# Filler gate weights of a hybrid encoder block: high and low parts made by GpSimd's converting and accumulating DMAs and a negated copy, instead of a load, a ScalarE copy and a VectorE subtraction

## The chip, the cores and the metric

The kernel runs on one core of a Trainium2 chip. A core has a matrix engine (TensorE, PE in the profile, with its weight loads as PEld), VectorE (DVE), ScalarE (ACT), GpSimd (POOL) and SyncE (SP), which here only issues DMAs. The engines work in parallel, each through its own instruction queue in order, and wait for one another by semaphores. The metric is the device time of one execution in microseconds (us).

## What is computed

One layer of an encoder with 1024 tokens and model width 1024, in float32. The reference, cut to what matters here:

```python
hn = rms_norm(x, norm_mix_g)
u = hn @ w_in                               # w_in: 1024 x 7864
u_mla, u_fox, u_ssm, u_gate = jnp.split(u, split_at, axis=-1)
y_a = mla_branch(u_mla, ...) @ w_br_mla     # attention, 8 heads
y_b = fox_branch(u_fox, ...) @ w_br_fox     # attention with decay, 8 heads
y_c = ssm_branch(u_ssm, ...) @ w_br_ssm     # Mamba-2 scan in chunks
g = sigmoid(u_gate + b_gate).reshape(B, S, 3, D)
x = x + (g[:, :, 0] * y_a + g[:, :, 1] * y_b + g[:, :, 2] * y_c) @ w_out
x = x + conv_ffn(rms_norm(x, norm_ffn_g), ...)
```

The part at issue is `u_gate`: 1024 tokens by 3 x 1024 gate columns, of which the last 3072 columns of `w_in` are the weights.

## The kernel before

**Arithmetic in two parts.** TensorE works on a rounded float32 type, `fp32r`. To keep float32 accuracy every operand `a` is split into a high part `h`, which is `a` rounded to `fp32r`, and a low part `l = a - h`. A product takes three matmuls, high by high, high by low, low by high. `hnh` and `hnl` are the two parts of the normalised input, transposed, in halves of 512 tokens; `wh` and `wl` are those of the weights.

**The stages, in order.** Projections (0 to some 380 us of the profile), the convolution's products with two pairs of gate blocks and a last single block, the bridge (L1481, to 531.8 us), attention of the 16 heads (to some 872), the chunk-wise SSD scan (to some 1066), the three branches' output products (L2328), the output product, and the gated MLP.

**The filler.** The gate columns come in 24 blocks of 128. Four are done earlier; the other 20 are the filler: a generator, `all_fill`, hands out their matmuls (L1588) in small groups that are placed between the matmuls of attention and of the scan, so that TensorE has work while the other engines do softmax and scan steps. A block is 48 matmuls of 128 x 512, in two halves of 512 tokens, each ended by a tanh on ScalarE (L1566) and, after the second, a store by SP (L1598). Per block of the rows `k = 0 .. 7`, the order is `wh·hnh`, `wh·hnl`, `wl·hnh`: the third matmul of a block is the first that reads `wl`.

**Loading a block.** `fill_load` is called for block n+1 when block n begins. It takes a raw buffer (`wr`), starts one 512 KB load on SP (L1552), and plans a ScalarE copy that rounds into `wh` (L1559) and a VectorE subtraction into `wl` (L1560). `wh` and `wl` have two buffers each, so the buffer of block n+1 is the one that block n-1 has used. The raw buffers, two as well, come free earlier: their load can run while TensorE still reads the `wh` of the same turn. The first two blocks are loaded with `now=True`, before the first attention matmul, with the helper `split` (L134, L135).

**What sets the order.** In attention the order on PE, ACT, DVE and POOL is worked out at build time by a planner (`Sim`): a list of tasks, each with an engine, the time for which it occupies it, the time until its result is there, and the tasks it follows. In this mode `later(us, fn, eng, cost, after)` adds such a task. In the scan only PE's order is written by hand; `later` then puts its work at so many microseconds of the builder's own clock behind the call, and the framework's scheduler orders ACT, DVE and POOL, with `pin` keeping those filler instructions in program order. GpSimd's own work in attention is the normalisation of the softmax rows (`pm`, L1926), between the exponential on ScalarE (L1918, with its row maximum `nmx` and reciprocal `rs` on DVE) and the transposes on PE (`tp`, L1966). In the scan it is, for each chunk, two products (`xdd` L2127, `y` L2129) and a chain of eight small operations for a reciprocal root (`yv` L2196 to `yr` L180). `xdd` is split by ScalarE (`xddh`) and VectorE (`xddl`) for the next chunk's state product (`pst`).

## Time and profile before

| | us |
|---|---|
| median of 3 runs | 1977.04 (1975.92 to 1977.86) |
| the profiled execution | 1973.83 |
| its span | 1972.1 |
| PE busy | 1949.2 (99%) |
| DVE, ACT, POOL busy | 1401.0, 976.9, 699.9 |
| TensorE clock granted | 0.999 |

The span is the time from the first to the last instruction of the profiled execution. Busy times are sums over instructions; matmuls are pipelined and their ends modelled, so that neighbouring ones overlap (one of 128 x 512 is listed at 390 ns, and the next starts 227 ns later). Instructions that issue a DMA aren't counted as busy. A wait is put down to the releaser that came last. In timelines the columns are the start, the duration, the engine, the line and what it writes and reads, and in brackets the idle time ahead of it with its releaser.

### The profile page before, as it was taken

The numbers are of one execution on the slowest core, as the hardware profiler recorded it, in microseconds if no ns is written. First come the engines' busy times: TensorE is split into PE (matmuls) and PEld (weight loads), VectorE is DVE, ScalarE is ACT, GpSimd is POOL, SyncE is SP. The second block draws the span as 40 slices with busy tenths as digits, with TensorE's granted clock in tenths as the row PEclk, the third lists the DMA queues.
The fourth block names the chain that finished last, engine by engine and source line by source line (L and its number), as shares of the span: only waits on it lengthen the run. The fifth ranks groups of instructions, "written<-read, shape, count | busy, mean of one in ns | idle before, by whom it ended". The sixth has DMA issues, their size and how long they took to land.

```text
span 1972.1 us, 28446 instructions
## 1 busy us (share of the span) xinstructions
PE 1949.2 (99%) x10053; PEld 1658.6 (84%) x10053; DVE 1401.0 (71%) x2178; ACT 976.9 (50%) x1690; POOL 699.9 (35%) x666
## 2 busy tenths in 40 slices
PE   9999999999999999999999999999999999999999
PEld 8989878888899988887888888888878888888887
DVE  7777769579566676758884575568997877765555
ACT  5555324454566666657783222225544444444432
POOL 5133100166133333213331451102664454423665
PEclk9999999999999999999999999999999999999999
DMA  6166755532757666635646875434222211259575
GB/s 181 53 198 212 202 132 155 187 102 91 227 167 195 177 179 169 170 95 194 214 152 228 291 252 184 139 107 127 94 90 86 76 53 54 86 166 337 185 262 191
DMA packets 281673, 318.46 MB, mean 161 GB/s; under 512 B 19405, under 2 KB 209497, under 8 KB 281530
## 3 DMA queue, kind: packets, MB, share of 16 engines
q1 hardware_dynamic: 281528, 316.64, 51.6%
q8 instruction: 79, 1.29, 0.3%
q14 instruction: 64, 0.52, 0.1%
q10 hardware_dynamic: 2, 0.00, 0.0%
HBM read 223.46 MB, written 93.13 MB: 161 GB/s over the span
## 4 chain that ended last, share of the span: by engine, by line
PE 86%; DVE 5%; issue 3%; ACT 2%; DMA 2%; POOL 1%; SPq 1%; ACTq 0%; DVEq 0%; POOLq 0%
PE dn L2760 10%; PE mm L1588 10%; PE ybr L2328 7%; PE cb L1384 7%; PE ua L2419 6%; PE uc L2419 5%; PE ud L2419 5%; PE wo L2464 4%; PE s L1899 4%; PE fx L798 3%; PE fx L1134 3%; PE tp L1966 3%; PE ub L2419 2%; PE fxv L188 2%; PE py L2172 1%
## 5 line engine op out<-in xcount | busy, mean ns | idle before, releaser
L2760 PE MATMUL dn<-dr,dr 128*128 128x512 f32 x592 | 182.3, 389 | 0.0
L1926 POOL TENSOR_SCALAR pm<-pm,rs 128x128 f32<-128x128 f32 (+7 forms) x128 | 95.3, 747 | 227.1 <-DVE rs L1924 203.6
L1588 PE MATMUL mm<-hnh,wh 128*128 128x512 f32 x320 | 132.6, 414 | 0.3 <-ACT t L1566 0.3
L2760 PEld LDWEIGHTS dn<-dr,dr 128*128 128x128 f32 x592 | 111.2, 188 | 22.9
L1588 PE MATMUL mm<-hnh,wl 128*128 128x512 f32 x320 | 125.7, 393 | 0.0
L1918 ACT ACTIVATE pm<-s,nmx 128x128 f32<-128x128 f32 (+7 forms) x128 | 94.8, 741 | 61.6 <-DVE nmx L1913 52.3
L1588 PE MATMUL mm<-hnl,wh 128*128 128x512 f32 x320 | 125.2, 391 | 0.0
L2760 PE MATMUL dn<-dr 128*128 128x512 f32 x296 | 115.3, 390 | 0.0
L1974 DVE TENSOR_TENSOR ptl<-tp,pth 128x512 fp32r<-128x512 f32 (+1 forms) x160 | 96.8, 632 | 23.7 <-ACT pth L1970 22.4
L135 DVE TENSOR_TENSOR dr<-dr,dr 128x1024 fp32r<-128x1024 f32 x52 | 71.4, 1380 | 51.7 <-ACT dr L134 44.4
L135 DVE TENSOR_TENSOR wl<-S,wh 128x1024 fp32r<-128x1024 f32 x55 | 81.4, 1480 | 35.6 <-ACT wh L134 35.5
L1913 DVE TENSOR_REDUCE nmx<-s 128x1 f32<-128x128 f32 (+7 forms) x128 | 93.4, 748 | 16.0 <-PE s L1899 9.3
L2328 PE MATMUL ybr<-ah,wl 128*128 128x512 f32 x256 | 99.8, 390 | 0.7 <-DVE wl L135 0.7
L2328 PE MATMUL ybr<-al,wh 128*128 128x512 f32 x256 | 99.9, 390 | 0.0
L2328 PE MATMUL ybr<-ah,wh 128*128 128x512 f32 x256 | 99.7, 390 | 0.0
L134 ACT ACTIVATE wh<-wr 128x1024 fp32r<-128x1024 f32 (+1 forms) x47 | 42.4, 902 | 104.6 <-PE ybr L2328 41.2
L1970 ACT ACTIVATE pth<-tp 128x512 fp32r<-128x512 f32 (+1 forms) x160 | 82.7, 553 | 23.1 <-PE tp L1966 21.2
L134 ACT ACTIVATE wh<-S 128x1024 fp32r<-128x1024 f32 x55 | 58.3, 1059 | 67.4 <-PE uc L2419 45.9
L134 ACT ACTIVATE dr<-dr 128x1024 fp32r<-128x1024 f32 x52 | 54.9, 1060 | 71.8 <-PE dn L2760 52.9
L1966 PE MATMUL tp<-ident,pm 128*128 128x128 f32 x576 | 80.9, 273 | 0.2 <-POOL pm L1926 0.2
L135 DVE TENSOR_TENSOR wl<-wr,wh 128x1024 fp32r<-128x1024 f32 (+1 forms) x47 | 54.5, 1159 | 32.9 <-ACT wh L134 32.8
L2637 DVE SCALAR_TENSOR_TENSOR fa<-cg,pc_f,fa 128x1023 f32<-128x1023 f32 (+1 forms) x44 | 74.2, 1688 | 1.4 <-ACT fa L2632 1.4
(665 smaller groups left out, 6219.4 us busy)
## 6 DMA issues: line engine op xcount, KB each, us to landing
dr<-act_d SPq DMA_DIRECT2D x99, 256.0 KB
wr<-in_w_in_dram SPq DMA_DIRECT2D x35, 512.0 KB
raw<-in_w_in_dram SPq DMA_DIRECT2D x27, 512.0 KB
gl<-g_d SPq DMA_DIRECT2D x24, 512.0 KB
wr<-in_ffn_w_up_dram SPq DMA_DIRECT2D x23, 512.0 KB
ws<-in_ffn_w_down_dram SPq DMA_DIRECT2D x22, 512.0 KB
wsum_d<-ws SPq DMA_DIRECT2D x22, 512.0 KB
act_d<-fa SPq DMA_DIRECT2D x22, 512.0 KB
```

Of the source, the lines that this page charges most:

```text
L134: i = A.activation(h, src, AF.Copy) if he is A else he.tensor_copy(h, src)
L135: return i, le.tensor_sub(l, src, f32(h))
L1384: T.matmul(ps, a, b, start=first and i == 0, stop=i == 11, skip_group_check=not first)
L1588: T.matmul(ps, a[:, k, :], b[half][:, k, :], start=(k == 0 and i == 0), stop=(k == NK - 1 and i == 2))
L1913: V.reduce_max(r.nmx[:, 0:1], r.row, axis=AX, negate=True)
L1918: A.activation(r.p[:, 0:cols], r.row, AF.Exp, bias=r.nmx[:, 0:1], accum_out=r.rs[:, 0:1])
L1926: r.norm = Task("G", (d - 0.025, d), lambda: G.tensor_scalar(r.p[:, 0:cols], r.p[:, 0:cols], r.rs[:, 1:2], 0.0, op0=ALU.mult, op1=ALU.add) ...
L1966: T.transpose(x.pt[:, c * P:c * P + P], rows_[qi].p[:, k * P:k * P + P], ident)
L1974: V.tensor_sub(x.tl[:, :off], x.pt[:, :off], f32(x.th[:, :off]))
L2328: T.matmul(pss[half], w_[:, k, :], a_[k][:, hs], start=k == 0 and i == 0, stop=k == nk - 1 and i == 2)
L2419: T.matmul(ps, a, b, start=first and n == 0, stop=n == 11, skip_group_check=not first)
L2760: T.matmul(ps[m], a[:, ts_], b[:, 512:], start=first_ and j == 0 and q == 0, stop=j == NFH - 1 and q == 2, skip_group_check=not first_)
```

## The change

For each filler block the raw buffer, SP's load, and VectorE's subtraction go. GpSimd instead starts two DMAs that read the weights' DRAM columns and write `wh`, rounding to `fp32r` on the way, four rows `k` each (256 KB). ScalarE writes `-h` into `wl`. GpSimd then starts four DMAs, of two rows `k` each (128 KB), that read the same DRAM columns again and add them to `wl`, so that it holds `w - h`. In the first two blocks this is issued at once; in the others the two, the one and the four are tasks, each after the one before.

```diff
     def fill_load(c0, now=False):
-        raw, rl = f_wr.get()
-        SY.dma_start(raw, w_inv[:, :, c0:c0 + P])
+        src = w_inv[:, :, c0:c0 + P]
         h, _ = f_wh.get()
-        l, _ = f_wl.get()
+        l, rl = f_wl.get()
         if now:
-            split(h, l, raw)
+            for k in (0, 4):
+                G.dma_start(h[:, k:k + 4, :], src[:, k:k + 4, :])
+            A.activation(l, f32(h), AF.Copy, scale=-1.0)
+            for k in (0, 2, 4, 6):
+                G.dma_start(l[:, k:k + 2, :], src[:, k:k + 2, :], accum_op=ALU.add)
             rl[0] = None
             return h, l, rl
-        i = later(4.0, lambda: pin(A.activation(h, raw, AF.Copy)), "A", (0.95, 1.06))
-        rl[0] = later(5.3, lambda: pin(V.tensor_sub(l, raw, f32(h))), "V", (1.13, 1.22), [i])
+        hd = None
+        for k in (0, 4):
+            hd = later(0.5, lambda k=k: pin(G.dma_start(h[:, k:k + 4, :], src[:, k:k + 4, :])), "G", (1.3, 5.0), hd and [hd])
+        rl[0] = later(7.0, lambda: pin(A.activation(l, f32(h), AF.Copy, scale=-1.0)), "A", (0.95, 1.06), [hd])
+        for k in (0, 2, 4, 6):
+            rl[0] = later(9.0, lambda k=k: pin(G.dma_start(l[:, k:k + 2, :], src[:, k:k + 2, :], accum_op=ALU.add)), "G", (1.0, 5.0), [rl[0]])
         return h, l, rl
```

Behind the change lines are seven higher: L1588 is L1595 there, L1926 is L1933, L2127 is L2134.

GpSimd's queue at the start of attention. Before, the last sum of the convolution (`cv`) is followed by the normalisations:

```order
L1459 TENSOR_TENSOR cv_5760<-X_5746,e_1084_5692 128x512
L1926 TENSOR_SCALAR pm_5909<-pm_5909,rs_5910 128x128
L1926 TENSOR_SCALAR pm_5912<-pm_5912,rs_5913 128x256
L1926 TENSOR_SCALAR pm_5933<-pm_5933,rs_5934 128x384
L1926 TENSOR_SCALAR pm_5947<-pm_5947,rs_5948 128x512
```

Now the DMAs of the first two blocks stand between:

```order
L1459 TENSOR_TENSOR cv_5760<-X_5746,e_1084_5692 128x512
L1556 DMA wh_5865<-in_w_in_dram 128x4x128 x2
L1559 DMA wl_5866<-in_w_in_dram 128x2x128 x4
L1556 DMA wh_5874<-in_w_in_dram 128x4x128 x2
L1559 DMA wl_5875<-in_w_in_dram 128x2x128 x4
L1933 TENSOR_SCALAR pm_5915<-pm_5915,rs_5916 128x128
L1933 TENSOR_SCALAR pm_5918<-pm_5918,rs_5919 128x256
```

Twelve DMAs have moved ahead of the first `pm`; the third pair, `wh_5874`, is written to the buffer that the bridge's matmuls read last.

ScalarE's queue at the same place, before, from the last tanh of the convolution's gates (`cv`) to the first exponential (`pm`):

```order
L1467 ACTIVATE cv_5760<-cv_5760,pc_g 128x1024
L1484 ACTIVATE gb_5774<-cb_5775,pc_g 128x512
L134 ACTIVATE wh_5873<-wr_5871 128x1024
L1484 ACTIVATE gb_5774<-cb_5801,pc_g 128x512
L1918 ACT_TABLE_LOAD
L1918 ACTIVATE pm_5909,rs_5910<-s_5891,nmx_5899 128x128
```

and now:

```order
L1467 ACTIVATE cv_5760<-cv_5760,pc_g 128x1024
L1557 ACTIVATE wl_5866<-wh_5865 128x1024
L1484 ACTIVATE gb_5774<-cb_5775,pc_g 128x512
L1484 ACTIVATE gb_5774<-cb_5801,pc_g 128x512
L1557 ACTIVATE wl_5875<-wh_5874 128x1024
L1925 ACT_TABLE_LOAD
L1925 ACTIVATE pm_5915,rs_5916<-s_5897,nmx_5905 128x128
```

Both blocks' copies have moved back: the first behind the tanh of `cv`, the second to the place right ahead of the first exponential.

GpSimd's queue in the scan. Before, the end of one chunk's chain (`yr`), the next chunk's products, and the next chain's first operation:

```order
L180 TENSOR_SCALAR yr_2552_11387<-rg_t_11396,yr_2552_11387 128x1
L179 TENSOR_SCALAR rg_t_11399<-yr_2552_11387,rg_v_11391 128x1
L180 TENSOR_SCALAR yr_2552_11387<-rg_t_11399,yr_2552_11387 128x1
L2127 TENSOR_TENSOR xdd_11558<-xT_11432,dend 128x1024
L2129 TENSOR_TENSOR y_11560<-xT_11432,Db 128x1024
L2196 TENSOR_SCALAR yv_2607_11607<-yss_11604 128x1
```

Now, at a chunk of the scan's first half:

```order
L180 TENSOR_SCALAR yr_2505_11190<-rg_t_11202,yr_2505_11190 128x1
L1567 DMA wl_11094<-in_w_in_dram 128x2x128 x4
L1564 DMA wh_11318<-in_w_in_dram 128x4x128 x2
L2134 TENSOR_TENSOR xdd_11363<-xT_11235,dend 128x1024
L2136 TENSOR_TENSOR y_11365<-xT_11235,Db 128x1024
L2203 TENSOR_SCALAR yv_2564_11413<-yss_11410 128x1
```

Six DMAs stand between the chain and `xdd`; from the fourth block of the scan on it is the two of `wh` that stand there, and the four of `wl` stand behind `y`.

## The prediction

> **What bounds the kernel now.** First the page: the busy line and the chain of waits.

> ```profile
> span 1972.1 us, 28446 instructions
> PE 1949.2 (99%) x10053; PEld 1658.6 (84%) x10053; DVE 1401.0 (71%) x2178; ACT 976.9 (50%) x1690; POOL 699.9 (35%) x666
> PE 86%; DVE 5%; issue 3%; ACT 2%; DMA 2%; POOL 1%; SPq 1%; ACTq 0%; DVEq 0%; POOLq 0%
> ```

> TensorE is without work for 1972.1 - 1949.2 = 22.9 us in all, so no relief of another engine can win more than that. The change touches the stretch in which the filler runs, attention (about 530 to 870 us) and the SSD scan (870 to 1070). Next, therefore, the waits of PE in those two windows:

> ```profile
> PE o L1978 <- DVE o L1950: 1.0, 4, 0.3
> PE s L1899 <- ACT pm L1918: 0.4, 2, 0.2
> PE tp L1966 <- POOL pm L1926: 0.2, 1, 0.2
> ...
> PE pst L2146 <- DVE xddl L135: 2.0, 1, 2.0
> PE stp L2104 <- issue: 1.3, 1, 1.3
> PE mm L1588 <- ACT t L1566: 0.3, 1, 0.3
> ```

> The columns are total us, times, longest. They add up to 5.2 us in 540 us: here TensorE alone sets the pace, and only 1.0 + 2.0 = 3.0 us hang on DVE, the engine that the change relieves. The other engines by window (us of PE, PEld, DVE, ACT, POOL, then clock, DMA share, GB/s):

> ```profile
> 650.00:700.00 50.00, 49.25 (x328) 44.41 (x326) 35.79 (x73) 33.90 (x75) 20.86 (x23) 1.00 0.67 187
> 950.00:970.00 20.00, 20.00 (x118) 17.30 (x117) 17.29 (x25) 16.26 (x36) 7.48 (x11) 1.00 0.65 198
> ```

> In attention GpSimd is free for 29.1 of 50 us; in one scan chunk of 20 us DVE is free for 2.7, ScalarE for 3.7 and GpSimd for 12.5.

> **What is removed.** For each of 20 blocks:

> ```profile
> L1552 SPq DMA_DIRECT2D wr<-in_w_in_dram x20: 373/384/592, 496.3 to 1011.9; - x20
> L1559 ACT ACTIVATE wh<-wr x18: 1042/1052/1069, 571.1 to 1038.4; 128x1024 fp32r<-128x1024 f32 x18
> L1560 DVE TENSOR_TENSOR wl<-wr,wh x18: 1205/1216/2928, 572.2 to 1045.7; 128x1024 fp32r<-128x1024 f32 x18
> ```

> DVE loses 20 x 1.216 = 24 us and SP 20 x 0.38 = 8 us, both beside TensorE's work. ScalarE keeps one pass of about 1.05 us per block, the negated copy, of the same size. What of it is on the path shows at the first scan chunk, where `pst` waited 2.0 us for `xddl`:

> ```profile
> 892.01 2.93 DVE L1560 TENSOR_TENSOR wl<-wr,wh 128x1024 fp32r<-128x1024 f32 x1
> 894.86 2.12 DVE L135 TENSOR_TENSOR Cl<-bc,Ch 128x256 fp32r<-128x256 f32 x1
> 896.90 1.21 DVE L135 TENSOR_TENSOR xddl<-xdd,xddh 128x1024 fp32r<-128x1024 f32 x1
> ```

> The subtraction stands two places ahead of `xddl`; without it the wait goes: **-2 us**, bounds 0 and -3. Of the 1.0 us in attention I count nothing.

> **What is added: 120 DMAs that GpSimd issues in its own queue.** Nothing like them is in the trace. Per issue on GpSimd I bound their time by SP's 0.38 us below, and above by the whole transfer:

> ```profile
> 879.15 3.50 DMA bc<-xbc_d
> ```

> This is a 256 KB load on the chain, as large as one of the two `h` pieces: 3.5 us to landing. If an issue can go out only when the one before has been drained, it costs about that. I take 1.1 us. It is the mean, weighted two to four, of what the new code books for GpSimd (1.3 and 1.0). The old code's bookings for the two removed operations, 1.06 and 1.22 us, agree with the rows above, 1.052 and 1.216, which is why I trust the new ones. From the end of an issue to landing I take 3.5 - 0.4 = 3.1 us.

> [...]

> **Place 1: the start of attention.**

> ```profile
> 531.79 1.06 ACT L134 ACTIVATE wh<-wr 128x1024 fp32r<-128x1024 f32 x1 [4.57 <-PE cb L1481]
> 533.44 1.28 ACT L1918 ACT_TABLE_LOAD   x1
> 535.37 0.37 ACT L1918 ACTIVATE pm<-s,nmx 128x128 f32<-128x128 f32 x1 [0.65 <-DVE nmx L1913]
> 536.13 0.37 POOL L1926 TENSOR_SCALAR pm<-pm,rs 128x128 f32<-128x128 f32 x1 [19.82 <-DVE rs L1924]
> 536.85 0.47 POOL L1926 TENSOR_SCALAR pm<-pm,rs 128x256 f32<-128x256 f32 x1 [0.34 <-issue]
> 537.81 0.49 PE L1966 MATMUL tp<-ident,pm 128*128 128x128 f32 x3
> ```

> The second block's `wh` buffer comes free only when the last bridge matmul (L1481) has read it, at 531.8. Before, the raw weights were already in another buffer. Now the transfer itself waits for that buffer, and GpSimd's queue holds both blocks' twelve DMAs ahead of the first normalisation. So: 531.8 + two `h` issues 2.2 + landing 3.1 + negated copy 1.06 + four `l` issues 4.4 = 542.6 for the first `pm`, not 536.1. ScalarE's first exponential also stands behind the copy (538.2, then 1.28 of table load), but ends before that. The second `pm` ends 1.2 us later, 543.8; the transposes then start 6.0 us late, and TensorE's order is fixed: **+6 us**. With 0.38 per issue the copy ends at 536.7 and the exponential sets the time: 538.0 for 535.4 before, of which 0.5 were spare (the second `pm` ended at 537.3), so 2.1. With 3.5 per issue and landing within the issue it is 531.8 + 7 + 1.06 + 14 + 1.2 - 537.8 = 17. The first block hides: its buffer is free at 515.4, and its copy stands behind the last tanh,

> ```profile
> 515.42 1.06 ACT L134 ACTIVATE wh<-wr 128x1024 fp32r<-128x1024 f32 x1 [1.90 <-PE cb L1384]
> 521.86 1.16 ACT L1467 ACTIVATE cv<-cv,pc_g 128x1024 f32<-128x1024 f32 x1 [2.05 <-DVE cv L1461]
> 531.93 2.72 PE mm L1588 x12
> ```

> so 523.0 + 1.06 + 4.4 + 3.1 = 531.6 is its last landing, before its first matmul at 531.9. The first slice lands 3.3 us before the last and is needed first, so some 4 us more are covered.

> **Place 2: the body of attention.** Eight loads of six DMAs, 48 x 1.1 = 53 us of GpSimd in some 340 us, beside TensorE; a `pm` that comes while an issue runs is up to 1.1 us late. The planner spaces the six among the normalisations, and PE's wait for `pm` was 0.2 us, so fill stands between. I count **+3 us**, bounds 0 and 15 (about a third of the issues uncovered).

> **Place 3: the scan.** In the changed order three blocks have their four `l` DMAs behind the reciprocal-root chain of the chunk. The rows of one such chunk before (the last from the chain of waits in order of time, the others from the timeline):

> ```profile
> 944.67 0.27 POOL L180 TENSOR_SCALAR yr<-rg_t,yr 128x1 f32<-128x1 f32 x1
> 944.89 2.92 POOL L2127 TENSOR_TENSOR xdd<-xT,dend 128x1024 f32<-128x1024 f32 x1
> ...
> 949.10 1.05 ACT L134 ACTIVATE xddh<-xdd 128x1024 fp32r<-128x1024 f32 x1
> ...
> 946.44 2.75 PE mm L1588 x12
> ```

> By the changed PE order a block starts half a block later than before, here at 946.4, and its first `wl` matmul is third, at 946.9. The first `l` lands at 944.9 + 1.1 + 3.1 = 949.1: 2.2 us of wait, the next slices (1.1 apart, needed every 1.4) none. Three blocks: **+6.6 us**, bounds 0 and 18. The same DMAs stand ahead of `xdd`: six issues, 6.6 us, so `xddh` on ScalarE moves from 949.1 to 955.3, with the next exponentials queued behind it. ScalarE has 3.7 us to spare in a chunk, so 2.5 us are late, for two chunks, and 0.7 for one with only four issues ahead: **+5.7 us**, bounds 0 and 15. From the fourth block on only two issues stand ahead of `xdd`; 2.2 us fit into the 3.7. The last block's negated copy stands behind the tanh of half a block before, 5.5 us ahead of its use, and the way is 0.7 + 1.06 + 1.1 + 3.1 = 5.9: **+1 us** with the later slices, bounds 0 and 3.

> **Sum.** -2 + 6 + 3 + 6.6 + 5.7 + 1 = +20.3 us on the profiled execution's own 1973.8 us: 1994. The runs' median, 1977.0, lies 3.2 above that execution, so I forecast **1997 us**. All lower ends, with -3 for DVE, give -0.9; all upper ends, with 0 for DVE, +68: 1976 to 2045.

> **The rivals.**

> A, cheap issues. If GpSimd only starts the transfers, as SP does in 0.38 us, place 1 costs 2.1, place 3 about 2, and DVE gives back 2: near 1979 us. For it: SP's row. Against it: the new code's own bookings. [...]

> B, each issue holds GpSimd until earlier descriptors have been drained. At 2.5 us each, between the ends: place 1 531.8 + 5 + 1 + 1.06 + 10 + 1.2 - 537.8 = +12. A chunk then asks 7.5 + 15 = 22.5 us of GpSimd against 20: 8 x 2.5 = +20, the three blocks' waits twice as long, +15, attention +5, tail +3, DVE -2: 1977 + 53 = 2030 us. For it: the pieces are cut small, four and two of eight rows. Against it: in attention they are apart.

> C, faster. The waits that DVE sets go (3.0 us), those for `issue` and the tanh too if engines run ahead (1.6), and no new wait appears: 1977.0 - 4.6 = 1972.4. It decides at place 1: the first two `pm` must end by 537.8, so the twelve DMAs must be through by 536.6. That leaves 536.6 - 531.8 - 1.06 = 3.7 us for six issues and one landing; even six of SP's 0.38 and a landing of 3.1 take 5.4.

> D, the accumulation lands late, over 8 us after its issue, since it must read its target as well. Then every scan block waits; the time is near B's, and it shares B's chance.

> **How the numbers follow.** Forecast 0.62, own range 1984 to 2015; A 0.17; B with D 0.14; C 0.07. About 0.2% (4 us) is what a measurement of this kernel tells from no change. Faster by more is C alone, 0.07; within it is A, 0.17; slower is the forecast and B, 0.76. The range 1978 to 2032 takes in the forecast, most of A and of B.

> **What would show it.** In the changed profile: twelve DMA issues on POOL around 515 to 543, and in the waits of PE a new one of about 6 us of `tp` for `pm`, at 538. PE waits of some 2 us of `mm` for a DMA or `wl`, three times between 915 and 970. On ScalarE a gap ahead of `xddh`. DVE's busy time lower by 24 us, POOL's queue carrying the issues. If PE shows no wait at 538, the issue's price is wrong, and A holds; if issues back to back are 2 us and more apart, B. If PE's busy time itself rises, TensorE's order costs something that I have put at nothing.

## The result, and the profile after

The changed kernel takes 2199.01 us (median of four runs, 2195.04 to 2200.92), the kernel before 1976.73 (1975.92 to 1977.86): a ratio of 1.1121, 95% interval 1.1102 to 1.1141, or 222 us more. The forecast was 1997, the upper end of its range 2032.

Some lines of the changed kernel's page:

```profile
span 2197.6 us, 28609 instructions
PE 2016.4 (92%) x10053; PEld 1697.2 (77%) x10053; DVE 1375.2 (63%) x2158; ACT 977.4 (44%) x1690; POOL 823.8 (37%) x786
q0 software_dynamic: 42880, 20.98, 7.3%
```

To see how much each stage lost, here is the busy time of the engines in four stretches (start, end and length of the stretch, then PE, PEld, DVE, ACT and POOL, the granted clock of TensorE with 1.00 as full speed, the share of the DMA engines, GB/s). POOL's busy time includes its DMA issues, 120 of them in the changed kernel; only those of the other engines are left out. The bounds are the first filler matmul, the first transpose of attention, the first of the scan, and the first of the branch projections. Before:

```profile
531.80:537.80 6.00, 6.00 (x31) 5.12 (x30) 2.75 (x6) 3.93 (x7) 0.84 (x2) 1.00 1.03 273
537.80:881.40 343.60, 341.22 (x2269) 302.43 (x2268) 232.38 (x485) 223.83 (x504) 120.32 (x146) 1.00 0.60 161
881.40:1066.10 184.70, 181.33 (x1003) 155.21 (x1002) 136.20 (x183) 133.18 (x278) 57.18 (x79) 0.99 0.57 185
1066.10:1972.10 906.00, 898.95 (x3989) 742.48 (x3987) 624.30 (x657) 367.93 (x443) 369.43 (x224) 1.00 0.47 159
```

and in the changed kernel:

```profile
536.70:580.10 43.40, 11.53 (x31) 7.86 (x30) 2.36 (x7) 6.13 (x11) 11.71 (x13) 0.60 0.43 76
580.10:976.50 396.40, 356.19 (x2245) 312.31 (x2246) 222.62 (x473) 223.23 (x500) 171.86 (x196) 0.95 0.63 148
976.50:1291.70 315.20, 226.11 (x1027) 179.16 (x1026) 119.30 (x174) 133.29 (x280) 116.11 (x138) 0.83 0.54 125
1291.70:2197.60 905.90, 898.95 (x3989) 742.29 (x3987) 625.92 (x657) 368.26 (x443) 371.94 (x224) 1.00 0.48 160
```

| stage | before | after | forecast | measured |
|---|---|---|---|---|
| start of attention (place 1) | 6.0 | 43.4 | +6 | +37.4 |
| body of attention (place 2) | 343.6 | 396.4 | +3 | +52.8 |
| scan (place 3; the -2 of DVE lies here too) | 184.7 | 315.2 | +13.3 | +130.5 |
| everything behind | 906.0 | 905.9 | 0 | -0.1 |

The filler's matmuls are shared out otherwise: in the changed kernel 24 of them, some 5.4 us at 227 ns, lie in the scan and not in the body (2245 for 2269, 1027 for 1003), so with the same work in each the two losses are about 58 and 125. The rest of the 225.5 us between the two spans, 4.9, lies ahead of the first filler matmul; that point moves between 531 and 537 us in the runs below as well, and I did not follow it up. In the three stages TensorE is busy 65 us longer with the same matmuls (593.8 for 528.6), at a lower clock; the other 155 us are waits.

GpSimd's timeline at the start of attention shows the reason ("issue" in the brackets is nothing that the profile shows):

```profile
521.22 1.01 POOL L1556 DMA_DIRECT2D wh<-in_w_in_dram  x1
528.64 0.77 POOL L1556 DMA_DIRECT2D wh<-in_w_in_dram  x1 [6.41 <-issue]
542.48 1.24 POOL L1559 DMA_DIRECT2D wl<-in_w_in_dram  x1 [13.06 <-ACT wl L1557]
547.23 1.23 POOL L1559 DMA_DIRECT2D wl<-in_w_in_dram  x1 [3.51 <-issue]
551.00 1.19 POOL L1559 DMA_DIRECT2D wl<-in_w_in_dram  x1 [2.55 <-issue]
...
578.42 1.22 POOL L1559 DMA_DIRECT2D wl<-in_w_in_dram  x1 [2.56 <-issue]
579.20 1.85 POOL L1933 TENSOR_SCALAR pm<-pm,rs 128x128 f32<-128x128 f32 x3
```

### The profile page after: what moved, and what is told of

Its sections match the earlier page's. It is cut to its first block, busy times and chain, and to the rows that moved or that the text cites. A ratio compares the mean times of both kernels' runs of the same rounds, so it can differ in the third digit from the quotient of the medians.

```text
span 2197.6 us, 28609 instructions
## 1 busy us (share of the span) xinstructions
PE 2016.4 (92%) x10053; PEld 1697.2 (77%) x10053; DVE 1375.2 (63%) x2158; ACT 977.4 (44%) x1690; POOL 823.8 (37%) x786
## 3 DMA queue, kind: packets, MB, share of 16 engines
q0 software_dynamic: 42880, 20.98, 7.3%
## 5 line engine op out<-in xcount | busy, mean ns | idle before, releaser
L1595 PE MATMUL mm<-hnh,wl 128*128 128x512 f32 x320 | 136.9, 428 | 56.1 <-DMA wl<-in_w_in_dram 55.7
L1567 POOL DMA_DIRECT2D wl<-in_w_in_dram x72 | 88.2, 1224 | 202.6 <-issue 118.6
L1933 POOL TENSOR_SCALAR pm<-pm,rs 128x128 f32<-128x128 f32 (+7 forms) x128 | 100.5, 831 | 111.7 <-DVE rs L1931 101.7
L1595 PE MATMUL mm<-hnh,wh 128*128 128x512 f32 x320 | 141.1, 441 | 0.9 <-DVE o L1957 0.9
L1595 PE MATMUL mm<-hnl,wh 128*128 128x512 f32 x320 | 133.7, 418 | 0.0
L1595 PEld LDWEIGHTS mm<-hnh,wl 128*128 128x128 f32 x320 | 65.1, 204 | 81.9 <-DMA wl<-in_w_in_dram 42.6
L1973 PE MATMUL tp<-ident,pm 128*128 128x128 f32 x576 | 86.5, 283 | 23.1 <-POOL pm L1933 23.0
L135 DVE TENSOR_TENSOR wl<-S,wh 128x1024 fp32r<-128x1024 f32 x55 | 82.0, 1492 | 34.9 <-ACT wh L134 34.9
L135 DVE TENSOR_TENSOR dr<-dr,dr 128x1024 fp32r<-128x1024 f32 x52 | 70.2, 1359 | 52.7 <-ACT dr L134 41.8
L1973 PEld LDWEIGHTS tp<-ident,pm 128*128 128x128 f32 x576 | 68.7, 145 | 28.5 <-POOL pm L1933 27.1
L134 ACT ACTIVATE wh<-S 128x1024 fp32r<-128x1024 f32 x55 | 58.3, 1059 | 67.6 <-PE uc L2426 45.8
L134 ACT ACTIVATE dr<-dr 128x1024 fp32r<-128x1024 f32 x52 | 55.0, 1061 | 71.6 <-PE dn L2767 51.8
```

The costliest lines, as they stand in the source:

```text
L134: i = A.activation(h, src, AF.Copy) if he is A else he.tensor_copy(h, src)
L135: return i, le.tensor_sub(l, src, f32(h))
L1567: rl[0] = later(9.0, lambda k=k: pin(G.dma_start(l[:, k:k + 2, :], src[:, k:k + 2, :], accum_op=ALU.add)), "G", (1.0, 5.0), [rl[0]])
L1595: T.matmul(ps, a[:, k, :], b[half][:, k, :], start=(k == 0 and i == 0), stop=(k == NK - 1 and i == 2))
L1933: r.norm = Task("G", (d - 0.025, d), lambda: G.tensor_scalar(r.p[:, 0:cols], r.p[:, 0:cols], r.rs[:, 1:2], 0.0, op0=ALU.mult, op1=ALU.add) ...
L1973: T.transpose(x.pt[:, c * P:c * P + P], rows_[qi].p[:, k * P:k * P + P], ident)
```

## The experiments

Each figure behind a + is the median less that of the kernel before on the same chip.

### Where the time is lost: the new transfers in one place only

```diff
+    def fill_load(c0, now=False):
+        return (load_accum if now else load_split)(c0, now)
```

Here `load_accum` is the changed function and `load_split` the old one. In the second kernel the condition is "planned inside attention", in the third "in the scan".

> The converting and accumulating transfers only for the first two filler blocks (twelve DMAs around the start of attention); the other eighteen blocks are loaded as before, by SP, ScalarE and DVE. Theory H (GpSimd holds each DMA until the one before it has landed, 3.8 us each, and what stands behind it in its queue waits): the first transposes come 37 us later than before, as in the changed kernel, and nothing after it: 1977 + 37 = 2014 us, 2005 to 2022. Rival L (the loss is a backlog that builds up over all twenty blocks, and the start pays little by itself): below 1990 us.

> The new transfers only for the eight blocks that are planned inside attention; the first two and the ten of the scan as before. Theory H: the 53 us by which the body of attention grew in the changed kernel, 1977 + 53 = 2030 us, 2010 to 2045. Rival L (backlog of the first two blocks carried through attention): below 1995 us, since the backlog is not there at the start.

> The new transfers only for the ten blocks of the scan; the first two and the eight of attention as before. Theory H, with GpSimd's queue as the bound of this stage (ten blocks of six DMAs at 3.8 us, with its own work): the 130 us by which the scan grew, 1977 + 130 = 2107 us, 2085 to 2125. Rival L (the scan pays for transfers that attention left behind): below 2050 us.

Measured: 2013.51 us, +38.5 (ratio 1.0197, 1.0182 to 1.0213); 2028.54, +53.6 (1.0278, 1.0253 to 1.0303); 2074.64, +99.7 (1.0504, 1.0488 to 1.0519). The first is the start's own loss in the changed kernel, so no backlog of all twenty blocks stands behind that. The second agrees with the body's +52.8 partly by luck, since its total is not all in the body. Its rows for the body and the scan:

```profile
539.70:923.70 384.00, 350.73 (x2246) 308.56 (x2245) 223.08 (x476) 223.84 (x502) 170.91 (x194) 0.96 0.64 155
923.70:1120.60 196.90, 187.53 (x1027) 159.92 (x1026) 140.47 (x184) 134.82 (x280) 56.07 (x79) 0.98 0.55 174
```

The body grew by 40.4 and the scan by 12.2 (24 matmuls, 5.4 us, have moved there as well). The scan alone came out at 100 for 130, between the ranges of the two theories. It holds only nine blocks with the new transfers, not ten, as its list of DMAs shows, with two for each block:

```profile
wh<-in_w_in_dram POOLq DMA_DIRECT2D x18, 256.0 KB, 3.3
```

The second kernel has eight, so one of the twenty blocks has the new transfers in none of the three. They add up to 192 of the 222. By the stages, some 10 of the other 30 lie in the body and 20 in the scan; at 11 us a block the missing one would account for about 11 (an estimate, 99.7 / 9). The rest comes up only where the stages follow one another, and I did not pin it down.

### Is the hold a matter of room?

```diff
-    nc = _bacc.Bacc(..., dynamic_dma_scratch_size=1024)
+    nc = _bacc.Bacc(..., dynamic_dma_scratch_size=1216)
-    top.tile([P, 56], F32, name="top", tag="top")
```

> The changed kernel with 1216 bytes in place of 1024 for the descriptors of GpSimd's DMAs (an unused tile of 224 bytes per partition goes for it). Theory R (a DMA is held since the memory of its queue has room for one of them only, and 1216 bytes are room for two): issues come in pairs about 1 us apart, a pair each 3.8 us, so a block asks some 12 us of GpSimd in place of 23, and the time falls to about 2070 us, 2030 to 2110. Rival Q (the queue takes the next DMA only when the one before has landed, whatever room there is): issues 3.8 us apart as before, 2199 us, 2185 to 2210.

Measured: 2059.96 us, +85.0 (1.043, 1.0412 to 1.0447). GpSimd's timeline of this run, from the first block's low part on:

```profile
532.00 2.49 POOL L1558 DMA_DIRECT2D wl<-in_w_in_dram  x2 [9.38 <-ACT wl L1556]
543.46 2.43 POOL L1558 DMA_DIRECT2D wl<-in_w_in_dram  x2 [8.97 <-issue]
...
553.73 2.46 POOL L1558 DMA_DIRECT2D wl<-in_w_in_dram  x2 [4.34 <-ACT wl L1556]
557.62 2.44 POOL L1558 DMA_DIRECT2D wl<-in_w_in_dram  x2 [1.43 <-issue]
```

The DMAs go out in pairs (x2), the last two pairs 3.9 us apart. The time is within the range of theory R. The total even hides some of the gain. In this kernel the stage behind the scan, which has no filler DMA, takes 14.5 us more than in the changed kernel, at the full clock:

```profile
1140.40:2060.80 920.40, 914.41 (x3989) 742.65 (x3987) 630.71 (x657) 368.88 (x443) 368.97 (x224) 1.00 0.47 157
```

TensorE is busy longer there with as many matmuls. The halved DMAs with 1216 bytes show the same (920.2), with 1024 bytes they do not (907.4), so it came with the larger room or the missing tile; why stays open.

The same test from the other side, with pieces of half the size, and half the booking for each (the cut shows the first two blocks):

```diff
-            for k in (0, 4):
-                G.dma_start(h[:, k:k + 4, :], src[:, k:k + 4, :])
+            for k in (0, 2, 4, 6):
+                G.dma_start(h[:, k:k + 2, :], src[:, k:k + 2, :])
...
-            for k in (0, 2, 4, 6):
-                G.dma_start(l[:, k:k + 2, :], src[:, k:k + 2, :], accum_op=ALU.add)
+            for k in range(8):
+                G.dma_start(l[:, k:k + 1, :], src[:, k:k + 1, :], accum_op=ALU.add)
```

> The changed kernel with each of its DMAs cut in two: four of two rows for the high part and eight of one row for the low part, twelve for a block in place of six, 1024 bytes for the queue's descriptors as in the changed kernel. Theory R (room decides): a DMA takes half the room, so two or three are under way at a time, 1 to 1.9 us apart on average, a block asks 12 to 23 us of GpSimd: 2110 us, 2060 to 2190, not slower than the changed kernel. Rival Q (one DMA at a time, whatever its size): twelve times 3.8 us, 45 us a block: above 2400 us.

> The same halved DMAs with 1216 bytes for the descriptors. Theory R: up to four of them at a time, so the whole way of a block through GpSimd's queue is 12 to 15 us: 2060 us, 2030 to 2110, about as with whole DMAs and 1216 bytes. Rival Q: above 2400 us.

Measured: 2111.13 us, +136.0 (1.0686, 1.0666 to 1.0707), and with 1216 bytes 2096.96, +121.8 (1.0603, 1.0586 to 1.062). GpSimd's timeline with 1024 bytes:

```profile
538.12 2.71 POOL L1559 DMA_DIRECT2D wl<-in_w_in_dram  x3 [9.07 <-ACT wl L1557]
543.87 0.87 POOL L1559 DMA_DIRECT2D wl<-in_w_in_dram  x1 [3.04 <-issue]
```

and with 1216:

```profile
520.99 3.17 POOL L1555 DMA_DIRECT2D wh<-in_w_in_dram  x4
532.12 3.62 POOL L1558 DMA_DIRECT2D wl<-in_w_in_dram  x4 [7.96 <-ACT wl L1556]
542.16 0.86 POOL L1558 DMA_DIRECT2D wl<-in_w_in_dram  x1 [6.42 <-issue]
```

So one whole DMA or three halves go out in 1024 bytes, and two whole or four halves in 1216, before the next is held: the idle time ahead of it is 3.5 and 3.0 us, 9.0 and 6.4 us for the low parts at the start of attention; the high parts there show the same counts with 1024 bytes (6.4 and 5.2 us). Room decides, and the queue does not take one DMA at a time by itself. If the bytes are simply shared out, these counts put a whole DMA above 512 bytes and at 608 at the most, a half above 256 and at 304 at the most (an estimate). The packets do not tell the room. Two DMAs of the high part alone make 1056 packets of the software queue (the changed kernel, 521 to 541 us), and one of the low part 272 (the run with every other block of the scan, 1008 to 1017.6 us), which is 33 and 17 for each of 16 engines; 40 x 16 x 33 + 80 x 16 x 17 are the 42880 of the changed kernel's page. Yet in 1024 bytes one whole DMA of either kind leaves no room for the next. Why half the packets take as much room was not shown.

Both times with halves are within the range of theory R, but with 1216 bytes 37 us above its 2060. Half a DMA does not cost half an issue: in the rows above four of the high part take 3.17 us, 0.79 each, as long as a whole one (0.79 at the median in the changed kernel), and three and four of the low part 2.71 and 3.62, 0.90 each for 1.22. So GpSimd is busy for 158.8 us in the scan (928.4 to 1176.5), with whole DMAs and the same room (920.1 to 1140.4) for 115.8. That this makes up the 37 us is my reading, which no run tests.

### The first block alone

```diff
+        return (load_accum if now and c0 == first_c0[0] else load_split)(c0, now)
```

> The new transfers for the first filler block alone, all others as before. My prediction let this block hide altogether: 1975 to 1980 us. Theory H (its two high parts land 20 us after the first issue, among SP's transfers, and four accumulating DMAs of 3.8 us each follow, with the first normalisation behind them in the queue at 550 us for 536 before): +14 us, 1989 us, 1983 to 1997.

Measured: 1989.02 us, +14.1 (1.0069, 1.0053 to 1.0085). GpSimd's timeline:

```profile
516.44 1.01 POOL L1571 DMA_DIRECT2D wh<-in_w_in_dram  x1
523.47 0.78 POOL L1571 DMA_DIRECT2D wh<-in_w_in_dram  x1 [6.01 <-issue]
535.60 1.25 POOL L1574 DMA_DIRECT2D wl<-in_w_in_dram  x1 [11.36 <-ACT wl L1572]
...
548.47 1.22 POOL L1574 DMA_DIRECT2D wl<-in_w_in_dram  x1 [2.62 <-issue]
549.25 1.30 POOL L1952 TENSOR_SCALAR pm<-pm,rs 128x128 f32<-128x128 f32 x2
```

The block that I had called hidden costs 14 us: 18 us to the last landing of its high part (the copy of 1.06 us stands between it and 535.6), then four held DMAs, and the first `pm` behind them.

### What the scan pays for

GpSimd's waits in the scan of the changed kernel, and ScalarE's:

```profile
POOL wl L1567 <- issue: 101.4, 33, 6.8
POOL wh L1564 <- issue: 42.6, 16, 5.9
POOL wl L1567 <- ACT wl L1565: 27.4, 7, 9.4
...
ACT y L2206 <- POOL yr L180: 66.0, 7, 13.8
```

With its 116.1 us of work, its own DMA issues included, the first three take up 287.5 of GpSimd's 315.2 us: its queue looked like the bound. Two tests, each from the kernel with the new transfers in the scan only; in the first, every other block has them (five of the nine), in the second, the chunk's reciprocal root is on DVE:

```diff
+        new = not now and sim[0] is None
+        turn_s[0] += new
+        return (load_accum if new and turn_s[0] % 2 else load_split)(c0, now)
```

```diff
-            G.tensor_scalar(v, ss, 1.0 / D, EPS, op0=ALU.mult, op1=ALU.add)
+            V.tensor_scalar(v, ss, 1.0 / D, EPS, op0=ALU.mult, op1=ALU.add)
...
-            rsqrt_pool(pool, r, v)
+            rsqrt(pool, r, v, 1)
```

> As the run with the new transfers in the scan only, but for every other block of the scan alone (five of ten; the others are loaded as before). Theory B (GpSimd's queue is the bound of the scan: a block with the new transfers takes it 27 us, of which 3.8 us are held behind nearly every DMA, against the 18.5 us of a block on TensorE): two blocks ask 27 + 8 = 35 us of GpSimd against 37, so the queue is no longer the bound and most of the 100 us goes: 1995 us, 1980 to 2012. Rival N (each DMA has its price, wherever it stands, and the prices add up): half of the 100 us stays, 2025 us, 2015 to 2035.

> As the run with the new transfers in the scan only, with the chunk's reciprocal root (yv and yr) on DVE in place of GpSimd, so that it doesn't stand behind held DMAs. Theory B (the queue's throughput): GpSimd has some 3 us a chunk less to do, eight times, so the scan shrinks by some 24 us: 2050 us, 2040 to 2062. Rival W (what costs is the wait of ScalarE for yr, 68 us of idle time in the scan): the wait goes, and 40 us and more of the time with it: 2035 us or less.

Measured: 2038.7 us, +63.7 (1.0321, 1.0301 to 1.0342), and 2067.22, +92.3 (1.0464, 1.0446 to 1.0481). All four forecasts fell: five of the nine blocks cost two thirds of the 100 us, and the root is worth 7. The first is just above the range of rival N, and five ninths of 99.7 are 55 for a measured 63.7. GpSimd's timeline of the first of the two, a chunk with new transfers:

```profile
992.68 0.83 POOL L1579 DMA_DIRECT2D wh<-in_w_in_dram  x1 [0.36 <-PE stp L2131]
...
1008.09 1.23 POOL L1582 DMA_DIRECT2D wl<-in_w_in_dram  x1 [2.64 <-issue]
1017.66 1.21 POOL L1582 DMA_DIRECT2D wl<-in_w_in_dram  x1 [8.34 <-issue]
...
1022.83 0.18 POOL L2223 TENSOR_SCALAR yv<-yss 128x1 f32<-128x1 f32 x1
...
1050.93 0.83 POOL L1579 DMA_DIRECT2D wh<-in_w_in_dram  x1 [0.36 <-PE stp L2131]
```

From one such chunk to the next, two blocks on, it is 58.3 us (1050.93 - 992.68), for some 37 before (184.7 for ten blocks). GpSimd has slack over the two, but in the chunk itself the root `yv` comes 30 us after the first of six DMAs, behind them all. So I took the queue's average to be the wrong view, and the place within the chunk to count. The test of that moves the root to DVE there:

> As the run with every other block of the scan (+64 us), with the chunk's reciprocal root (yv and yr) on DVE in place of GpSimd. There GpSimd has slack over two chunks, but in a chunk with new transfers yv and yr stand behind six held DMAs, and DVE (48 us) and ScalarE (50 us) wait for them. Theory O (that order within a chunk is what costs): with the root out of GpSimd's queue most of the 64 us goes: 1998 us, 1985 to 2015. Rival D (the low parts landing late for TensorE, or xdd behind the DMAs, cost by themselves): most of it stays, 2025 us and more.

Measured: 2012.95 us, +38.2 (1.0189, 1.017 to 1.0208). The time is within theory O's range, but its reason is half right: 25.5 of the 63.7 us were the root behind the DMAs, not most of them. Of what is left, the row of its scan, in the columns above, and TensorE's longest wait there show the kind:

```profile
882.70:1104.30 221.60, 194.96 (x1003) 162.88 (x1002) 147.72 (x242) 136.03 (x278) 63.06 (x45) 0.92 0.61 166
...
PE mm L1615 <- DMA wl<-in_w_in_dram: 18.9, 8, 4.1
```

18.9 us are waits for the low part, and at a clock of 0.92 the same matmuls keep TensorE busy for 13.6 us more than before (194.96 for 181.33). That the root was worth only 7 us where all nine blocks are new I read as the queue being full there: its work ran while the next DMA was held anyway. That reading was not tested.

### Converting alone, and the landing

Against the changed kernel, the lines of the first two blocks (the others likewise):

```diff
-            A.activation(l, f32(h), AF.Copy, scale=-1.0)
-            for k in (0, 2, 4, 6):
-                G.dma_start(l[:, k:k + 2, :], src[:, k:k + 2, :], accum_op=ALU.add)
+            V.tensor_sub(l, raw, f32(h))
```

with SP's load of `raw` as before; and then without it:

```diff
-        raw, _ = f_wr.get()
-        SY.dma_start(raw, src)
+        raw = f32(hnh[0][:, :, 0:P])
```

> Only the high parts by converting DMAs, two a block; the low part by the old subtraction on DVE from raw weights that SP loads (ScalarE has no copy of the filler any more). Theory H (each DMA on GpSimd costs its hold, whether it converts or accumulates): four DMAs in place of twelve ahead of the first normalisations, +15 us there; a third of the 54 us of attention, +18; the scan, no longer bound by GpSimd, +10: 2018 us, 2000 to 2040. Rival A (the accumulating DMAs, which read their target as well, are what costs): within 8 us of before, 1967 to 1985.

> As the run with converting DMAs only, without SP's twenty raw loads of 512 KB: the subtraction reads another resident tile in their place, so the low parts are left out of the result. Theory S (a DMA of GpSimd lands late, and so holds the queue longer, while SP's transfers are on the same DMA engines): the median landing of the high parts falls from 4.5 us towards 3.6, the long ones of up to 13.5 us are fewer, and at least 15 of the 70 us go: 2015 to 2030 us. Rival P (a DMA of GpSimd has its price whatever SP does): 2040 to 2050 us.

Measured: 2044.89 us, +69.7 (1.0352, 1.0339 to 1.0365), and 2053.58, +79.5 (1.0395, 1.0377 to 1.0413). So it is not the accumulation alone: rival A is out, and with a third of the DMAs a third of the loss is left. Theory H missed by 5 us above its range. Its first two terms came out (the start of attention takes 20.5 us for 6.0, the body 362.3 for 343.6), but the scan takes 221.8 us for 184.7, +37 for its +10 (5.4 of it are 24 matmuls that moved there from the body). There DVE, which makes the low part from the high part, waits for late landings. Its longest wait between the start of attention and the end of the scan, in the run with the load of `raw`:

```profile
DVE wl L1565 <- DMA wh<-in_w_in_dram: 38.9, 9, 12.7
```

Theory S fell: without SP's raw loads the median landing is 4.7 us, with them 4.5, and the time is no better (+79.5 for +69.7), above rival P's range too. The holds do go with the load on the DMA engines. Of the 52 DMAs of the changed kernel that follow another with nothing between and nothing to wait for, 38 started within 4.2 us (share of the DMA engines 0.44 on average), and 11 after 5 us and more (0.85). Two rows of the run with every other block of the scan show it, for the two DMAs that start at 1008.1 and 1017.7 us:

```profile
1008.10:1017.60 9.50, 5.25 (x28) 4.16 (x26) 2.30 (x3) 4.61 (x10) 1.22 (x1) 0.98 0.77 228
1017.70:1021.50 3.80, 3.71 (x16) 3.08 (x16) 0.00 (x0) 0.00 (x0) 1.17 (x1) 0.61 0.33 36
```

Whether the other transfers cause it, and which, stays open: only the raw loads are ruled out.

### What the relief of DVE was worth

```diff
-            split(h, l, raw)
+            A.activation(h, raw, AF.Copy)
...
+        rl[0] = later(4.0, lambda: pin(A.activation(h, raw, AF.Copy)), "A", (0.95, 1.06))
+        return h, h, rl
```

The lines behind this `return` are no longer reached.

> The kernel before without the low parts of the filler's weights: DVE's twenty subtractions are left out, and the third matmul of each step reads the high part. What the relief of DVE can bring at the most, if nothing takes its place. My term was -2 us, 0 to -3: 1973 us, 1970 to 1977. Rival V (DVE's queue sets more of the kernel than the waits show): 1960 us or less.

Measured: 1979.07 us, +3.9 (1.0021, 1.0013 to 1.003). Both forecasts fell. Without the twenty subtractions and with nothing in their place the kernel is not faster. The wait from which I had read the -2 us is still there:

```profile
896.86 1.21 DVE L135 TENSOR_TENSOR xddl<-xdd,xddh 128x1024 fp32r<-128x1024 f32 x1
PE pst L2148 <- DVE xddl L135: 2.7, 1, 2.7
```

`xddl` starts at the same point as before (896.90): other operations of DVE now stand ahead of it. The change had nothing to win here, so I did not look for a version of it that beats the kernel before.

## Why the prediction was wrong

**The step that failed** is the price of an issue on GpSimd's queue, 1.1 us. I named the right end ("If an issue can go out only when the one before has been drained, it costs about that", 3.5 us) and took 1.1, from what the new code books. For the issue itself that is right: 0.80 us for 36 DMAs of the high part and 1.22 for 72 of the low part make 1.08 on the mean of a block. But a DMA behind another is held until that one has landed, 3.9 us from start to start at the median and up to 8.1, and the booking says nothing of that: I had put the hold at nothing. The runs with other room and other sizes show that it is a matter of room.

**Rival B** ("each issue holds GpSimd until earlier descriptors have been drained") is what happened, and I gave it, with D, 0.14. Its size was off as well, 53 us for 222. It took 2.5 us for a hold of 3.9; with 3.9 in its own sum, place 1 would be 21, the scan's chunks 8 x 10.9 = 87, and the whole about 129 us (an estimate). It also counted the scan as an average, what a chunk asks of GpSimd beyond its 20 us. The run with every other block showed that this is not the whole sum: order within the chunk and the late low parts cost where the average has slack. **D**, late accumulation, is not it: the median landing is 3.6 us for both kinds. **C** is out, and so is **A**: its 0.4 us an issue is below the 0.8 to 1.2 measured, and it leaves out the hold.

**Place 1**, +6 forecast, +37.4 measured. The order of the queue was right: `pm` behind twelve DMAs, the copy ahead of the first exponential. Wrong were the hold, and "the first block hides", worth 14 us by itself: I gave its landing 3.1 us, and its second high part took over 12.

**Place 2**, +3 forecast, +52.8 measured. "A `pm` that comes while an issue runs is up to 1.1 us late" holds for one DMA; where two follow each other, `pm` is behind the hold, and TensorE waits. Its largest sum of waits in that stretch of the changed kernel:

```profile
PE tp L1973 <- POOL pm L1933: 23.0, 11, 9.0
```

**Place 3**, +13.3 forecast, +130.5 measured. `xdd` and the low parts are waits that I named, but `yr` was not among the late ones in my sum: I looked only at what stands behind the chain, not at the chain behind the next block's DMAs. The term for `xdd` has a slip too: by the rows it moves to 944.9 + 6.6 + 2.9 = 954.4, not 955.3, which makes 3.9 us of the 5.7 and changes little.

**DVE**, -2 forecast: this term was wrong too. I took the subtraction ahead of `xddl` for the reason of `pst`'s wait, but without it the wait is 2.7 us for 2.0 and the whole 3.9 slower. That attention's body is shorter there,

```profile
540.90:880.70 339.80, 336.71 (x2245) 298.22 (x2244) 223.20 (x476) 222.66 (x502) 119.34 (x146) 1.00 0.58 163
```

is no gain: it has 24 matmuls less (2245 for 2269), which lie in the scan instead.

**TensorE's own time** I had put at nothing, and named it as what would make the prediction wrong. It is 65 us of the loss, at a lower clock.

**DVE did not hold the DMAs.** In a stretch of the changed kernel at the start of attention,

```profile
543.00:566.00 23.00, 8.27 (x22) 5.87 (x22) 0.72 (x2) 0.61 (x2) 5.87 (x6) 0.57 0.41 68
```

DVE is busy for 0.72 us of 23, and DMAs that follow one another are 3.5 to 3.9 us apart all the same.

## What to carry to other kernels

Before moving loads to GpSimd, count in a trace how many of its DMAs go out before one is held: here there was room for one, each waited out the whole landing of the one before (3.6 us at the median), and everything in order behind it on GpSimd's queue paid. Count what stands behind a held DMA in each round of a loop, not only the average load of the engine. And look whether the engine that is to be relieved sets anything at all: a run without its work, with nothing in its place, tells that before the change is written.

## What the hardware showed beyond that

TensorE loses more than the wait. Rows of the changed kernel, TensorE's timeline around its first long wait, and the stretch behind it:

```profile
536.97 0.39 PE L1595 MATMUL mm<-hnl,wh 128*128 128x512 f32 x1
547.05 0.77 PE L1595 MATMUL mm<-hnh,wl 128*128 128x512 f32 x1 [9.70 <-DMA wl<-in_w_in_dram]
547.61 0.63 PE L1595 MATMUL mm<-hnh,wh 128*128 128x512 f32 x1
...
547.00:555.50 8.50, 7.63 (x20) 5.68 (x21) 0.72 (x2) 0.00 (x0) 3.04 (x3) 0.51 0.28 31
```

After a wait of 9.7 us the matmuls start 0.43 us apart (the next one at 548.04) in place of 0.23, for some 8 us, at a granted clock of 0.51. In the scan the clock is 0.83 over the whole stage, and 226.1 us of matmuls (1027 of them) stand for 181.3 (1003). What brings the clock down was not shown.
